# First block's shift and scale from VectorE's sums in place of TensorE's one-column matmuls, with a new order of all instructions

## The chip, the core and the metric

The kernel runs on one core of a Trainium2 chip. The core has five engines with a queue of instructions each: TensorE (PE in the profile, with PEld for its weight loads), VectorE (DVE), ScalarE (ACT), GpSimd (POOL) and SyncE (SP), which issues nearly all DMA transfers. An engine takes its instructions in the order in which they were issued and stops at one whose semaphores are not yet there; everything behind it on that engine waits too. The metric is the device time of one execution in microseconds (us); the time of the kernel before is the median of three runs.

## The reference: what is computed

One layer of a decoder, for a single sequence of 512 tokens with 1024 channels and one conditioning vector c, in float32:

```
mod = silu(c) @ ada_w + ada_b                 # 6 x 1024: shift, scale, gate, twice
sh1, sc1, g1, sh2, sc2, g2 = split(mod, 6)
h = rms_norm(x, g) * (1 + sc1) + sh1          # the modulated input of the mixer
y = hybrid_mixer(h)                           # RG-LRU branch and sparse attention
x = x + (1 + g1) * rms_norm(y)
h = rms_norm(x) * (1 + sc2) + sh2
y = square(relu(h @ w_ff1)) @ w_ff2           # 1024 -> 4096 -> 1024
x = x + (1 + g2) * rms_norm(y)
```

The change concerns the first two lines: how sh1 and sc1 are computed for the first 128 of the 1024 channels. Each is, per channel, a sum over 1024 products silu(c)[k] * ada_w[k, channel] and a bias.

## The kernel before

Every float32 weight is split into a high and a low part of the type fp32r (names hi_..., lo_...), the activations likewise (h, hl), and a float32 product is three fp32r matmuls into one PSUM bank: high by high, low by high, high by low. All matmuls are issued by one helper (L396), transposes by another (L400), ScalarE's operations at L407, those of VectorE and GpSimd at L441, loads on SyncE's queue at L483.

The order of the work is not that of the program text. The helpers only record each operation as a node, with the engines that could do it; `flush` then issues the nodes in the order that `PLAN` spells out, two characters a node. Where an operation can be done by more than one engine (a copy or an elementwise operation), `PLACE` says for each stage, letter by letter, which takes it: a for ScalarE, d for VectorE, p for GpSimd. Both strings are written out in the kernel. So each engine's queue, SyncE's with the loads too, has a fixed order across all stages. A load into a buffer that was used before waits until the last reader is through, and every load behind it on SyncE's queue waits with it.

The opening works in this order. `OPENING` loads the four tiles of x (128 tokens by 1024 channels each, 512 KB), six tiles of ada_w (512 KB, name p, from in_ada_a) and the first two weight blocks of the projection (384 KB, raw_a). The p tiles have six buffers, so the seventh load goes into the first one's buffer. TensorE runs 24 filler matmuls (stage WM) on x's first tile into a bank of the first wave, whose result nobody reads (name s). ScalarE squares and sums each x tile, GpSimd makes the reciprocal root, and x is scaled in column blocks of 128, 256 and 640 (stage XN; r<-r,stat in the profile). silu(c) lies as a column layout `sil` (128 x 8); eight float32 matmuls broadcast it over all 128 partitions into two PSUM banks (tp<-sil,ident), and two copies (the stage with the empty name in `PLACE`) make of them `silb`, 128 x 1024.

Then the eight blocks j of 128 channels follow in `first_wave`: `ada_sums(j)` gives the block's shift and scale as two columns `sa`; `ada_load(2)` loads two more ada_w tiles; four transposes turn the block of x; ScalarE makes h = scale * x + shift from the PSUM bank (for j = 0 in two halves of 256 tokens), once rounded to fp32r and once in float32 (pt), VectorE takes the difference hl; and 18 matmuls (stage MW: 3 terms by 6 column tiles of the projection) add it into six PSUM banks, f, f, s, s, pv, pv.

`ada_sums` has two forms. For j > 0 the two ada_w tiles lie transposed, channels on the partitions, and VectorE multiplies each with `silb` and sums along the row (tensor_tensor_reduce, shown as CUSTOM_DVE_ANT_0 p<-p,silb, with the read of its accumulator), followed by one small step for the scale. For j = 0 the two tiles lie the other way, and TensorE makes the sums: 16 float32 matmuls of one column for the shift and 16 for the scale, as the profile counts them (8 k-blocks, 2 records each), into the two banks pv that the wave uses later; a tensor_add and a scalar_tensor_tensor on VectorE (sa<-pv) finish them.

Behind the wave come the rest of the projections, the conditioning columns ar, the recurrent branch and the attention (to about 275 us), the output projection and residual, and the MLP in two passes over weights f and A, B (284 to 612 us).

Of the kernel before, what the change touches and what calls it, by code (L numbers as in the profile page):

```python
# [16 lines left out]
S = 512
D = 1024
NT = 4
KD = 8  # L20
# [75 lines left out]
    '2d372E2K2~2G3S2c2j2g2e2f382b2l2i333V3T2k39352r2h2n342/2m2q363W2*2p3X2%2o2-3*3!3U2,3x3#2<2]3c3Y2?2=3y3C3Z'
    '3I3$2:3a2{2@583d2^3O3F3D3z3b3%3e3h3&3J3n3+3P3(3L3i3o3,3R3)3t4#3k3/4H3?3u4%3:3q4F3{3@45463w3A473G3M484M2.'
    '3|3f4O494C3l3r4A3<4N4B3-4g3=4G4$4h4i4k4l4m4j4Q4^4&4n4P4+4o4,4-4]GY4(4.2+2>4~4S5L504)2;514*3]5K4/2[4_3~4{'
    '4d2_3^5Y3E413K3Q52425D3B5X5M4|4}59533H3j445E5h5A5B5C435F5H5G3N5g5J3p3v5O3g3m5I5N5S3;5$3[5P3s4b7%5T3.5R3>'
    '4a3_3}4J5Q5#5Z5U5V5a5b5i5j5k4I5-5W5l5m5d5n5o5p5q5,5r4X5s7&4V5t5u4K5e627)6;4c6-5v4L5w6<6.6/5x6=5y615z5f6d'  # L100
# [1709 lines left out]
```

## Time and profile before

| what | value |
|---|---|
| time, three runs | 627.72, 629.02, 629.98 us; median 629.02 |
| the profiled execution | 627.82 us, its span 626.0 us |
| mean granted TensorE clock in it | 0.991 |
| TensorE busy | 596.3 us (95%) |
| VectorE busy | 539.2 us (86%) |
| ScalarE busy | 346.1 us (55%) |
| GpSimd busy | 209.1 us (33%) |
| instructions in the profile | 9043 |

The span runs from the first to the last instruction; the time of the execution is a little longer. A row of a timeline gives the start and length of an operation in us, its engine and line, what it writes and reads, and in brackets the idle time of its engine just before it and what ended it. Operations of one engine overlap a little at their ends, so the distance from start to start is what one costs in a dense row of them, not the length.

### The profile page before, as it was taken

Reading aid. Unit: us, or ns where it says so; the run is one execution under the profiler, and the core shown is the slowest. Engines: PE = TensorE matmul, PEld = TensorE weight load, DVE = VectorE, ACT = ScalarE, POOL = GpSimd, SP = SyncE. Lnnn points to the kernel's source line nnn. Section 1 sums busy time; section 2 is a strip of 40 time slices with the busy share of each in tenths; the row PEclk is TensorE's granted clock in tenths of the full one; section 3 lists DMA queues with packets and bytes.
Section 4 is the critical chain, followed back from the end, with each engine's and each line's share of the span. In section 5 each row is a group of like instructions: output and inputs, shape, how many; then the busy total and the mean of one; then the engine's idle time right before and its main releaser. Section 6 shows DMA issues by size and latency. Waiting matters only on the chain.

```text
span 626.0 us, 9043 instructions
## 1 busy us (share of the span) xinstructions
PE 596.3 (95%) x3060; PEld 497.9 (80%) x3060; DVE 539.2 (86%) x1072; ACT 346.1 (55%) x696; POOL 209.1 (33%) x209
## 2 busy tenths in 40 slices
PE   7999999998999999989999999999999999999992
PEld 6888788966777898869887888888887888878881
DVE  5986988979999988988888968787688789999897
ACT  6654525698999999687251220322322247465563
POOL 5001301652663175453204547641351231000113
PEclk9999999999999999999999999999999999999997
DMA  8968895430503302015664334254544426756613
GB/s 351 416 250 318 320 299 191 131 136 1 202 2 129 141 2 102 1 35 176 229 222 168 115 133 137 101 169 157 180 135 147 155 69 204 238 179 202 198 56 134
DMA packets 29430, 102.15 MB, mean 163 GB/s; under 512 B 3268, under 2 KB 3524, under 8 KB 29384
## 3 DMA queue, kind: packets, MB, share of 16 engines
q1 hardware_dynamic: 29240, 101.50, 46.4%
q8 instruction: 24, 0.39, 0.3%
q14 instruction: 22, 0.18, 0.1%
q10 hardware_dynamic: 144, 0.07, 0.0%
HBM read 99.47 MB, written 2.10 MB: 162 GB/s over the span
## 4 chain that ended last, share of the span: by engine, by line
PE 73%; DVE 11%; DMA 6%; ACT 5%; issue 3%; DVEq 0%; SPq 0%; ACTq 0%
PE f L396 36%; PE s L396 14%; PE pv L396 13%; PE tp L396 7%; DMA ar<-in_ada_t 4%; PE tp L400 4%; DVE r L441 3%; ACT p L407 2%; DVE fT L441 2%; ACT r L407 2%; DVE ar L441 1%; DMA raw_A11l<-in_wd 1%; DMA raw_A10l<-in_wd 1%; DVE p L441 1%; DMA r<-in_x 1%
## 5 line engine op out<-in xcount | busy, mean ns | idle before, releaser
L396 PE MATMUL f<-h,hi_f 128*128 128x512 f32 x224 | 87.7, 392 | 0.0
L396 PE MATMUL f<-h,lo_f 128*128 128x512 f32 x224 | 87.2, 389 | 0.0
L396 PE MATMUL f<-h2l,hi_f 128*128 128x512 f32 x224 | 87.2, 389 | 0.0
L407 ACT ACTIVATE fT<-f 128x512 f32<-128x512 f32 x30 | 17.8, 594 | 71.2 <-PE f L396 71.2
L396 PEld LDWEIGHTS f<-h,hi_f 128*128 128x128 f32 x224 | 42.1, 188 | 8.8 <-issue 0.2
L396 PEld LDWEIGHTS f<-h2l,hi_f 128*128 128x128 f32 x224 | 42.0, 188 | 8.6
L396 PEld LDWEIGHTS f<-h,lo_f 128*128 128x128 f32 x224 | 42.0, 188 | 8.5
L396 PE MATMUL f<-hi_o,h 128*128 128x512 f32 x128 | 47.7, 414 | 0.0
L407 ACT ACTIVATE p<-p,mx 128x32 f32<-128x32 f32 (+4 forms) x96 | 45.1, 472 | 3.8 <-DVE mx L441 3.6
L441 DVE TENSOR_TENSOR lo_f<-raw_f,hi_f 128x1024 fp32r<-128x1024 f32 x29 | 40.1, 1383 | 6.9 <-ACT hi_f L407 6.6
L400 PE MATMUL tp<-ident,p 128*128 128x128 f32 x192 | 41.6, 273 | 1.9 <-DVE pt L441 0.9
L396 PE MATMUL pv<-pt,V 128*128 128x256 f32 x160 | 42.2, 316 | 1.1 <-ACT pt L407 0.7
L441 POOL TENSOR_SCALAR p<-p,den 128x32 f32<-128x32 f32 (+4 forms) x43 | 35.7, 863 | 18.5 <-DVE den L441 15.5
L396 PE MATMUL s<-K,Q 128*128 128x288 f32 (+4 forms) x128 | 38.4, 336 | 0.5 <-DVE Q L441 0.3
L441 DVE TENSOR_TENSOR pt<-tp,pt 128x512 fp32r<-128x512 f32 (+1 forms) x56 | 33.6, 609 | 3.3 <-ACT pt L407 1.9
L407 ACT ACTIVATE hi_f<-raw_f 128x1024 fp32r<-128x1024 f32 x24 | 24.9, 1056 | 18.7 <-PE f L396 13.0
L396 PEld LDWEIGHTS pv<-pt,V 128*128 128x128 f32 x160 | 27.8, 189 | 6.1 <-DVE pt L441 2.1
L396 PE MATMUL s<-r,fs 128*128 128x512 f32 x96 | 32.5, 389 | 0.0
L396 PE MATMUL pv<-r,fs 128*128 128x512 f32 x96 | 31.8, 391 | 0.4 <-DVE r L441 0.4
L400 PEld LDWEIGHTS tp<-ident,p 128*128 128x128 f32 x192 | 25.0, 140 | 7.8 <-issue 1.8
L396 PE MATMUL tp<-r,fs 128*128 128x512 f32 x96 | 30.6, 389 | 0.0
L441 DVE CUSTOM_DVE_ANT_0 ar<-ar,silb 128x1024 f32<-128x1024 f32 x16 | 21.6, 1352 | 6.4 <-DMA ar<-in_ada_t 6.4
(732 smaller groups left out, 1817.0 us busy)
## 6 DMA issues: line engine op xcount, KB each, us to landing
raw_f<-in_wf SPq DMA_DIRECT2D x32, 512.0 KB, 3.5
p<-in_ada_a SPq DMA_DIRECT2D x16, 512.0 KB, 8.0
ar<-in_ada_t SPq DMA_DIRECT2D x16, 512.0 KB, 4.4
ar<-in_ada_r SPq DMA_DIRECT2D x16, 512.0 KB, 4.0
r<-in_x SPq DMA_DIRECT2D x8, 512.0 KB, 4.6
raw_c<-in_wc SPq DMA_DIRECT2D x8, 512.0 KB, 5.2
raw_o<-in_wo SPq DMA_DIRECT2D x8, 512.0 KB, 6.4
raw_a<-in_wa SPq DMA_DIRECT2D x8, 384.0 KB, 7.5
```

The lines of the kernel that those rows point to most:

```text
L396: lambda: self.nc.tensor.matmul(out, lhs, rhs, start=start, stop=stop))
L400: self.issue("pe", 0.109, [out], [src], lambda: self.nc.tensor.transpose(out, src, ident))
L407: return "act", cost, lambda: self.nc.scalar.activation(out, src, func, scale=scale, bias=bias, **kw), func
L441: return eng, cost, lambda: fn(out, *args, **kw), None
```

## The change

`ada_sums` loses the branch for j = 0: the first block's shift and scale are two tensor_tensor_reduce and one small step on VectorE, like those of the other seven blocks. On the host the first two tiles of `ada_a` are laid out transposed like the others. The number of nodes goes from 4836 to 4821: sixteen matmul calls (32 records in the profile) and two VectorE operations fewer, three VectorE operations more.

`PLACE` and `PLAN` are made anew for the whole kernel. Counted over all free picks, ScalarE goes from 568 operations to 569, VectorE (with its fixed ones) from 938 to 961, GpSimd from 201 to 178. In the opening the two copies to `silb` go from VectorE to ScalarE, and of the twelve scalings of x six are ScalarE's, five VectorE's and one GpSimd's, where eleven were ScalarE's and one VectorE's. The new order puts on VectorE first the scale sum of block 0, then some scalings, the low part of the first weight block, the shift sum of block 0, and then the sums of blocks 1 and 2. The loads keep their order up to the fourth block of the next weights.

```
 PLACE = {
-    '': 'dd',
+    '': 'aa',
...
-    'XN': 'aaaaaadaaaaa',
+    'XN': 'paadaddddaaa',
...
 PLAN = (
-    '000O0P020Q0106400R0S0T0U0V0M074p4q084r0a0W0y040b4sGX4t090c030&0d0X0A554u0C4v054w0e4x0(0-4y0Y0H0N4z4!0D4:'
+    '000O0P020Q010M0R0S0T0N0U0V074a0B3:4b084c090a0y4d0W0A4e0C0b0&0c0X030d0e4f0z4g3}0-0H0Y4h044i0(0f054j0!0I4k'
...
         sa = const.tile([P, 2], F32, name=f"sa{j}")
         b, b1, pm = cols[:, V_AB + j:V_AB + j + 1], ab1[:, 8 + j:9 + j], cols[:, V_PM + j:V_PM + j + 1]
-        if j == 0:
-            w = [a.rearrange("p (k s q) -> p k s q", k=4, s=2) for a in ada[:2]]
-            to = [wave[4][:, 0:1], wave[5][:, 0:1]]
-            for k in range(KD):
-                for e in range(2):
-                    mm(to[e], w[k // 4][:, k % 4, e, :], sil[:, k:k + 1], k == 0, k == KD - 1)
-            dve("tensor_add", sa[:, 0:1], to[0], b)
-            dve("scalar_tensor_tensor", sa[:, 1:2], to[1], b1, pm, op0=ALU.add, op1=ALU.mult)
-        else:
-            for e, first in enumerate((b, 0.0)):
-                w = ada[2 * j + e]
-                dve("tensor_tensor_reduce", w, w, silb, 1.0, first, ALU.mult, ALU.add, sa[:, e:e + 1])
-            dve("scalar_tensor_tensor", sa[:, 1:2], sa[:, 1:2], b1, pm, op0=ALU.add, op1=ALU.mult)
+        for e, first in enumerate((b, 0.0)):
+            w = ada[2 * j + e]
+            dve("tensor_tensor_reduce", w, w, silb, 1.0, first, ALU.mult, ALU.add, sa[:, e:e + 1])
+        dve("scalar_tensor_tensor", sa[:, 1:2], sa[:, 1:2], b1, pm, op0=ALU.add, op1=ALU.mult)
         return sa[:, 0:1], sa[:, 1:2]
...
-    first = ada[:, :2 * D].reshape(KD, P, 2, KD, P)[:, :, :, 0, :]
-    ada_a = [first[k:k + 4].transpose(1, 0, 2, 3).reshape(P, 1024) for k in (0, 4)]
-    ada_a += [ada[:, e * D + j * P:e * D + j * P + P].T for j in range(1, KD) for e in range(2)]
+    ada_a = [ada[:, e * D + j * P:e * D + j * P + P].T for j in range(KD) for e in range(2)]
```

More of the change, by code (lines that the diff above doesn't have):

```diff
@@ L87 @@
-    'XN': 'aaaaaadaaaaa',
+    '': 'aa',
+    'AS': 'daapaaappdapaadapadpdppppapddapaapadpppadaddpdaadpdddaappadaapadppdadddpaappppppapppppppappdppap'
+        'appaaadpppapaaad',
+    'AV': 'aaaaadadddaddddaaddaaaaaaaaaaadaadadaaaaaaaaaaaadaaaaaad',
+    'AW': 'adaddaadpppddddd',
+    'DA': 'pdpddddadddpdddddddddppdddadddddpdadddddadppdappddddddpdddpappadpdpadpaddaddddddpadddpdpdddddpdd'
+        'ddddddpdppapdddapddddadddpapdddpaddppddddpdaddddaddaddddppddddapdddddddddaddaddd',
+    'DN': 'adadadadadadadadadddadadddadadadddadadadadadadadadadadadadadadadddppdddppddd',
@@ new lines @@
+    'FA': 'dddpddddpddd',
+    'RS': 'ppadddddadda',
+    'TH': 'daddaaddddddaaddddddaadpddddaadd',
+    'UP': 'ddppddpdddpddpddddpddpdddddddddd',
+    'VW': 'pdpddddddppdppppppp',
+    'WS': 'adadadadadadadadadadadapadadadapdpapadapddadddapadadadadaddaddadpadddddpaddaddadadaddadddddaddda'
+        'dddddaddapddaddadpaddadddaddadddddadddadpddpdddadaddddadpadddddpaddadpadddpddddddddaddddaddddadd'
+        'addadddaddddpdddddadaddaddaddddadadpaddaddadadaddaddadddddaddaddadddadadppadadddadadddadadddadad'
+        'ddadadddadadddddadddadadddadadddadadddadadddadadddadadddadadddadad',
@@ L96 @@
[L96 to L100, printed above, removed]
@@ new lines @@
+    '120q0%0^0r0s0t1U0u140|0v0}0+0w17131V0x181H1B0$1C1X1#151Y1E1Z1G1g1a1)1b1K1$1F1c1M1*1+1D1W1,161J1e1h1P1d1N'
+    '1Q1S1:1%0<1i1n1L1f1&1I1.1O1(2B271R1-1T1t1l2I1k1q061;2C1o2p1z2D1m261<2E1u1w1j1r1x1/291p1!2A1v2J1?1s1y281='
+    '2e2K2F1@1]1[2G2i1^2q1{1|1}242d2j1>22232N2k202f2H2g2l2:2;2m1~2h2-1_2L2r2n2O21252[2<2.2T2R2P2Q2X4@2=2o3G2M'
+    '2s2]2Z2S2u2W2/2U3D2^2>2Y2V3H2y2?3I2a3E2c3N2x2!2b2%3O2,302&2v3F3J2@3P3l2)3L2#3j2|363K2*3m2}3s3n3i343o3A33'
+    '393T3k3S4[3M3p2_313Y3t3q3Z3e3x3C3r3u3%3f4m3,403V3?374o3y3[3QGJ3&3b423-3@3h3_2t3W4]3]2w473{2$3!3c493^483|'
@@ new lines @@
+    '4R4S4T4n4V2z3v2(4W4A3#4*4X4)4U4p2+4Y4q4Z4r4C3*563)4E2{2~4B4t3/414u4N4v4w4/553<4s4:3;4x4+354,4D3B5J574;4-'
+    '4<4}4.4L3U5I4=4~4^4_4{50323=5S383R4|3>51523a543X3d5R593g3z3(535D7o583w5n7p3$5G5A3+3.5E5C5B5K4M5L5M7r5T44'
+    '5m5U5V4I5W5X5O5Y5H5v5Z5a5F5b4O5c5d5u435e5f6O5g5h465P6z5<5i5j5N456P6!6v5k4P5o5l6w6x6#4H5[5;5p7q6$4G6Q6+4F'
+    '5]5q685r676,6y6-6&5^4Q5_6G5{5|5Q4K6R5}6(4J5~5s606.616F5t62635w6S7$6b5x5y6a6)5z6*5!6/647%5+656j6T666%6<69'
+    '5,6A6B6C6D6U6E7-5#6V6W6i6X5$6H6I5%7;6;7L6Y5&5-6J7t6@6K6=7M5(5)6L6Z5*6:5.6c6[6d5/6N6e6|5:6>6M6f5=6g6{5>6h'
@@ new lines @@
+    '7C5?6?6]6k5@6^7D6l6_6m6n7N7&7k7Z7(787)777.6o7/6p7:7d6q7eGH7<7a6r7f7=7>7?6s7b7@7c7l7g7h7[7]7i7j6}7*867^6t'
+    '7u6~8G7m8O8P8H7v7_8I7+7{8M7w8K7|8Q708S8L7}718=8>728[7x8^738?748U8]9p857~758_80818~8N90768J7987GK91937A7z'
+    '8@7n897E7B8R7F8V8A6u9q7G8T8B7H9t8C7I7J928D7K7O958E7P968F7QGL8*949y7R7S9rG&7T8+9z7U8,8W978-9!8.8/9s8:G)8f'
+    '9u8;8g8h8i8X8j7V8k8l8<988b8{A99E8m8|8e8nG*8o8p8d8q8r7y8s999D8tG+8Y8u7s8}7!8ZAF7,9G8a7W9H8v8c8wG(9W9#AA7#'
+    '8x828y9X8z8!8#7X8$9c9I8%9Y9J9C9K9B9Z8&839LAG9d9M8(AH9N9e9O9PAD9a9g9h9f9i9Q9jAB9R9b9k9l9S9m9?AI9n9T9@Ag9A'
@@ new lines @@
+    '9o9F9~9v8)9[9UBwAh9w9V7Y9]9^9_AaAb9xAi9{A0BxA19$AcACAeA29%CMAE9}9&9(9)A39*AJ9+9,AKA5B^9-A4AwCNCO9|A$9.AN'
+    'CTAOBy9/HAALCUAdCV84AkAfAxB_9:A%Ca9;AlAmC8ARCbAnAQCcB{A!APCmASAyAT9<CnAoCoA&CtC9AjA6CuAUCvA7ApA}9=A;A(Cx'
+    'A~A8CyA#A?B4CzB2B6AVB0Aq88B3ArBeB5B1B7AzC!A<BfAsA)A=C#AMBAA>BCC+B8AtHBA@AWBgA*AuHMA/A.C$BhBuA:AXAvA-A^B;'
+    'BvAYA[HCA_CGB=A]A+B<A,AZA{BYHDCHA|BSBZBTBUBNB>BaBVC2BWCICBBbBXC4C3BcCFC6CCC5BOBmC7BiCDBdBnBjC,CKBkC&BoC('
+    'C-C/DGC:C;CEC<C=CPC>CSC)C@CJC[DHC]C^CLC_C{C|CfCQDIC}C~D0CWD1CZD2D3D4CXBlChD5BqCkBrBsD6D7CrC*9>ClD9CgDADB'
@@ new lines @@
+    'D8CeDnDCDoFSBtCsD&DDDEDtDFC%D(DJD)DKB9DLCiDfD*DMCYDNDOCpDgDSBDD+CdDTBBDUDjCqDuDrDVDhDWBEDpDPDXBpD,DlDYBF'
+    'DZCjBPD-DaDkCRDbDcC?DqDdDsD.D/DiBzB!DeC.B#EdD|DmEeEfBKD@DQBMEgBJD:D;FUB&D<DvBLB(B%D[D}BGEhDwCwEiEsEtBHB)'
+    'B*D#B-D=B+BILpD~EuFWE(D%D_B.E)E0E*D]GGB,ELEMCAD!E+B$E,ENLqEPE-E_G~ERFoEvESE{D$EQE|DxB/F3DzF4ETD{FYF5D>B:'
+    'FOEUBQFPBRFQD^D?H0E1FRB?EwE2EOB@B[FVE#EVDyE3H4EWE$EZEBDRE4E%EHH$HPECEcB]FCEzFDF-E5FZB|ExB}FEEIEaH%F6EJED'
+    'EbF7E6EXE7F.F/E8E9B~FAEAF8FpF=GuGvEKH8EEF:E>GwE?F!EFFTF#H5EjEGFXE@H&FuC0FvF>E.EkFyE/E:ElF;EYE;EmF$LrE[F@'
@@ new lines @@
+    'EnEoF+GFE<GiE]C1E=EpFaH6EyFwErFbGjE^FeFcFfFdFgFhEqGcGkGdFkFFFlGgFmG_G{E}FqF,FnFrGxFiFsF<GeF1G>GyFjGlF?F]'
+    'G?FtFzF^F_F{F|F}F9F2F~G]F[F&FBH(F(H)G|H*E&GzG0H1G@H9E!HaHbHmH+G^H,G8G1FGE~G9F)FHH-FJH2G}FKGAHeF*HnGBFLH.'
+    'GCG2HoHfH3GDG3G4FNHcG5IFFMHyG6HzHdH/H!G[G7I0IGGEHpGSGWI1GXGTGhGYGZHqGUHrGVGMGNGaHuGOGPH:HxGQGbH#G!FIHKGR'
+    'H;F0GfIJFxG,G#HNF%IKIHG$JDI2I4G-ILHOGmIrI5HwI%H7IlGnG%HLG.ImGsJEIIG:G;InJFIpGqG<IsG/I&GrG=ItI(I{HQHgI3HU'
+    'J6IuHVHhJGHRIqHiJHJIIoJ7HTHSJ8GtHWHEHFIvJ9H@HGHjJwJ2HkHXIwJAH[I$JBHYHlJxHJJyJCJzHZI|HtH<GoJ!HsJ%HHH^HIIB'
@@ new lines @@
+    'H_H=GpH{H]H>J#H?I6J$I7I}H|IAI8J&MgI9K9J0J(ICH}IMKAKBIDJ)H~MeIQKbJ*INJ+MWK2J3JeMYIEIRISIOJ4J1MZHvJkJfKcJg'
+    'IzIZIPJlITIUJ5K3JmIaIbIcIfMfK4IdJ|IgIhJiJ}IiIVIeKdIjKeI)JnKfMhJ]I-IWKgIkI*I~I.I+I,JhI/MXJ^JjI[I:KhJ~I;Ki'
+    'J_JoKjI!I=I>KkK1K5I?IYI]KTJ{I@JpIxKXI<JJI#KULDK0IXKYKVI^JKJSIyLEI_JvJsJTKxJUKZKyKWJYJLJVJMKzJtLFJWKaK(JZ'
+    'JNJOLSK#JPJaJuK)JXK|K!LTJbJRJ,LUJcK*J-J.LeK+J:JdK}L1LfK~L2K,J/J>JrKHJ?L3J;K-LaL5KIK<J<KJKKJ@L0LhJ=J[LiKL'
+    'KCL4LbLgK;LcKNKOKDKPK/LjLlKEKQJqLmLdJQK:LnKML:L;K6KRK7L>L?KpL<K8L@KSKlKmMNL=KqK=KnL[MOLoLGKGKoLHLIKrLkLJ'
@@ new lines @@
+    'KtKuKFKvMRKsK$LKMPK%K.KwL]MSK[K]LLLMK&K^LNLtL^LOMTLPL_LxMVLyL~LQLuMyK{LzK>L}LvLRM$L!M%MUK_LwL%L#M&L*MzM1'
+    'L+L,LVL&L-M!L(L)K?L$L.K@L6M0MBL/N2M|MCMDOaL7LYMFMGMELZL8MHL9MQM}MIN3M2N1OeM6MsM~MtM3ObMJMuMKM7MvMLMMM9LA'
+    'MwMnN4LBMAMoLWNdMxM4NhNiL|LCNeNlOfLXM<OiNjMjM@M[MkM=NfM>MpM)MaM(M*MlM+M,M8M?N*M]N.M-M^OjMbN0McN+M_M.L{M/'
+    'M:OcN/N,M;NEM#NPOdNQNLOgNFN-M{O7NRNMNNNSN:O&NTNGNOMrO(N5NVMqO)NUNWNZO*OkN6NHNXN7NYO+NANBNINJOlNaO8O,NbO-'
+    'O9NCN;OmO.NcNmOhNvOBO/OANwNKLsOCNnNgODNxMiN#NyOEN$NDNoMdN%O:NpNzN&PGNqPHN!N(PIPJO;NrPTM5N)N<N@N[N=N>N]N?'
@@ new lines @@
+    'OFN^O>O1N|N_PUO2N9O3N}NkN~O0N{O4N8PKNsO<PVOGPLO5O?OSOOOHPWNuOKOPO6OTOQPXOUORPYNtOLO=OWOVOsOXPZOIOYPaOMON'
+    'OtPbO@OZOuOvOnOyOwOzO!OoO#PMOxO$PcPNOpO{POO%P0O[P1O|O}OrP2P3PdPeP4PAPBO]PfPCPDO~O^PPPQP5P6PROJP7P8PSP9Mm'
+    'PuPEPqPrPvPsOqP<PgPwPtP=PFP$P%P>PxPyPhPzP!PkP#QAP&QBPjP?QCP@P(PiO_P)QEP*QDP+P[PlP]QFP^P,QGP_P{P|QIPmQOP-'
+    'QHP}P.QJP/P~QKPnP:PoQLP;Q(Q)Q*QMQ+Q0PpQiQjQ,QNQPQQQRQYQZQSQaQ-Q4QbQTQ]Q^Q3QVQ_Q{QcQ|Q1QUQ}Q2QdQ~QrQsQfQk'
+    'QtQuQ5QeQlQmQwQnQoQvQpQqQhQ6Q#QWQ$Q%QgQ.QXRAQ&Q7Q8QxR0RCQ/RBRDQ:Q;Q=Q<R4RERFRgQ>RhQzRiQ?R1RjQ@RGRkRlQ[Rm'
@@ new lines @@
+    'QyR2RnQ9RoRpQ!RqRrR3RsSHRtRuRHRvRwRxR+R,RJRLR-R.R/R5R:RIR;R<R=R~S0S1S2S3S4RKS5R6S6S7S8S9SASBSCSDT}SERVSF'
+    'SGSKSLSMR7SNT~SOSPR8RWSQSRSSSTSUU1SVSWR9SXSYSZSaSISbScSdSeU2SfSgShRMRNU0RORXRYRQRZSiSjU4SkRPSlSmSnSoRbSp'
+    'RRSqSrSsRaStRSSuSvRcSwSxRTSyRyRdRzR!ReR#SzS!RUR%S#R>S$U3R?R$S%S&R@R[RfS(U8R&S)R]S*S+S,SJR(S-R^S.S/S:R)S;'
+    'R_S<S=R*S>R{S?S@R|S[S]S^S_R}S{S|S}T>S~T0T1T2T/U9T3T?T4T5T6T7U5T8UAT9UBTATBUCTCTDTET@TFUETGUDTHT;TIU~URTJ'
+    'TKTLUST<UTTMTNUUV0T=UVU6TOUWT:UXUFTPU7TQUYT[V1TRTSTTUZTUTVUGUbTWUcTXUdTYUfT]VAUgULTZTaUhUjUkUMTbUlUnV5Tc'
@@ new lines @@
+    'UNTdUoVGTeUHTfUpUOTgThUqTiTjTkTlV2V6VBTmUPUyVaUzTnU!UIUQU#U$U%U(U)ToUaU*U+U,V7TpU-UeTqU.U/VbVCU:TrTsU;U<'
+    'TtUiU=VfU>U?UmU@U^TuVDV3UxTvVVTwVEUuTxTyV4TzU_UrT!T#UsVFUtUvT$VJU{VKWrUwU|VLT%T&T^VcWsT(VdUJVeVMVHVjUKVN'
+    'WwT)VkT*T_T+T,VOT-VlVgVmVnU&T.VoVqT{VrVhVsVPVvVwVxVIVzV!VQU[VZV#V(ViV)U}V*U]VRWGV+V,V-V;XOV.V<V=V>WHV?Xt'
+    'V@V[VpVSV]V^T|V_V{V|V~W0WxVTVtW1W3W4VWWIW5VuVUWJW8WXW9WAWBVyWCWDWRWyWEWSWTWUWtWuVXWvW!W#V:W$VYW%W&WKW(V}'
+    'W)W*W+WFW,W-W.W2W/W:W;V/WVWWW?W6W@W7W[W]W^XPW_WLW}W{V$W~X0X1XuX2X3X4X5X6XQX7X#X8WYX9WzWMXAXBXUXCWZXDXEXF'
@@ new lines @@
+    'XVXGW|XHXIXJWNXKWOXLX(WmXMX)X*YWX+X,YXX-X.WaX$X/X:X;WbX<V%X%X=X>X?X@X[X]Y#X&X^X}WcY$WdX~Y0Y1Y2XWY,Y3V&Y6'
+    'WqY7Y8Y9YAYBYCYDY-YEYFYGYHY4YIY.YJYKYLYMYNYZYOY/YPYYYQXRWeWfYRWnYSYTY:WoY;Y<WgZeY=Y>Z,ZfY?Y@XSXXY[Z?Y]Ya'
+    'Y^Z-Y_WhWiYUY{WjXNZ>Y|Y}WpY~XTWkYcWlZ0Z@XZZ1Z2Z6Z7YbZ[Z8XfZ9ZAZBZhZEZCZFXaY5YdXbZGZHXcZIXdW<ZJZKXeWPZLXg'
+    'YVXiXjXkXoZMZNZOYeXlamZPZQZiXmZgZRZSZTapZUZVZWWQZXXnZYXYZZZaZbZ]a}ZcXvZ^W=a>XwZ_anZ{ZjZ|a~Z}Z~a0Xxa1Zna2'
+    'b0a3ZDXya4a5Xha6a7Zka8Xsa9W>aAaEZlXza?aFaGaHaIaJawaMa|aKX!ZmaNXpasaOaPYhaQbuaRaSaTXqaUaVaWaXaYYiYnaZXrYj'
@@ new lines @@
+    'aaabacYkb|adaeafZdagahaiajYlb1Yfb2b3b4X_b5Ymb6b}X{b7b8YqYob9YrakYsYtc6bAYubBbCX|atbDbEaqYvV8Y%YpbFY&bGau'
+    'Y(Y)aobHYwbIY*bMc7Y!Y+Zpc5bNbOZqalZrc8ZsZtbxbPZubQarbRbyZybvbUbzYxZzbVbwbWbSZvbXbYbZb!baaLbbZ!bcYybdbebf'
+    'c$Yzbgd5bhbiZ#c+bjbkd6blbmZ$bnboc(dDbpZ%bqbrZ.bsc9cAcBbtcCcDcEZ3cFcGZ/V9Z4Z:dEcHcIb#cJbTcKZ;cLc%ZwcMZ<Z5'
+    'cNZ=cOdFcPcQaxcUcVc&dGcWZ&cXcYcZZxeDccaycdd:Z+ceb$cfZ(azeEcgcachcicjckZ)eLclcmcnd-Z*a!b%cocpc.a#b&cqa$cb'
+    'crcsctcua)cva%a*a+cwa,cxcyczdHaBa-dIdJdKdLdMYgdNdOdPa/dQdRdSa&dTeMdUdVdWa(a.dXa:dYeNa=dcddc!dea@c)a[avdf'
@@ new lines @@
+    'dgdhfLdkdidla]a;dmdndod.dpaCdqdraDdsdtc#dua<a^a_eOdjdvdwa{b.b(dxdydzd!d#c/d$d%d&Zob)d(d)bJd*b*ePc*eQb[eR'
+    'fUeSeTd/eUb+c,eVc-b,eWeXfVeYb-eZb/b;b<eabKb:ebecd+b=fMedeeb>efb?bLb@fTb~c0b{e?egekd;fWd=c1ele@c2b]emd,c3'
+    'enc4eoc:epb^c;esetgTd@eub_c<d>e~evewd?c=f}c>exe[eyg1eze!d<c?c^c_e]e#c{e$c@e%e&e(c|c}e)f0c~e*cRd7e+e,d0cS'
+    'e-d8e{eqe.d9dAc[e/cTdBe:e^e;ere<fXe=fYg8fZc]e|dCfagcd]d1fbd4d^d2d_d{fcd|fdfee_ffd3fgd}fhg4fie>fje2e3g2fk'
+    'gUfle4fme5fng3fogbe6d~e7fsdZfte0fueFe8f~fveGfwe1fxeHfyf!e9eCf#daf$f%gdf&eIf(eJf)dbgef*f+eAf,f-f.hCeKeBf/'
```

124 lines of the change are left out of this document (22 added, 102 removed).

## The prediction, made before the changed kernel ran

> **What bounds the kernel now.** I read the times of the engines first, then the table by stages, then the chain of waits, and last the rows of each engine around the change. The page of the profile:
>
> ```profile
> span 626.0 us, 9043 instructions
> PE 596.3 (95%) x3060; PEld 497.9 (80%) x3060; DVE 539.2 (86%) x1072; ACT 346.1 (55%) x696; POOL 209.1 (33%) x209
> ...
> PE 73%; DVE 11%; DMA 6%; ACT 5%; issue 3%; DVEq 0%; SPq 0%; ACTq 0%
> ...
> L407 ACT ACTIVATE fT<-f 128x512 f32<-128x512 f32 x30 | 17.8, 594 | 71.2 <-PE f L396 71.2
> ```
>
> TensorE is busy for 596.3 of 626.0 us and holds 73% of the chain that ended last. The profiled execution took 627.82 us, so 1.8 us lie around its span. The median of the three runs is 629.02; I work out a difference on the profiled execution and add it to the median. The three runs differ by 2.3 us among themselves, so 0.3% (1.9 us) is about what a measurement of this kernel tells from no change.
>
> The busy time by stages (columns: stretch, its length, then busy time and count of PE, PEld, DVE, ACT, POOL, the granted clock, the DMA share, GB/s):
>
> ```profile
> 10.36:18.61 8.25, 8.25 (x78) 8.25 (x76) 6.97 (x19) 6.99 (x14) 1.75 (x4) 1.00 1.04 421
> 18.61:46.15 27.54, 27.54 (x137) 22.25 (x136) 25.08 (x47) 16.75 (x24) 0.00 (x0) 1.00 0.83 323
> 46.15:100.00 53.85, 50.74 (x291) 43.00 (x291) 45.10 (x73) 22.60 (x37) 6.91 (x7) 1.00 0.85 303
> 100.00:275.00 175.00, 168.72 (x980) 139.75 (x980) 160.16 (x468) 154.32 (x390) 85.46 (x97) 1.00 0.24 85
> 275.00:284.00 9.00, 6.25 (x35) 5.81 (x36) 8.23 (x14) 7.85 (x12) 3.51 (x4) 0.81 0.21 65
> 284.00:612.00 328.00, 327.07 (x1516) 271.93 (x1516) 278.09 (x404) 127.69 (x200) 100.84 (x78) 1.00 0.48 161
> ```
>
> From 18.61 us, where the first projection matmul starts, to 46.15 TensorE has no gap at all, and VectorE is busy for 25.08 of 27.54 us. From 284 to 612 TensorE waits 0.9 us in all. It waits 3.1 us in 46 to 100, 6.3 us in 100 to 275, and 2.8 us in the hand-over to the MLP. The stretch of 8.25 us ahead of 18.61 looks full as well; the chain of waits shows with what (first its shares in 10.36 to 18.6, then two of its pieces with their start and length):
>
> ```profile
> by line: PE s L396 51.2%; PE pv L396 35.6%; PE tp L396 9.3%; PE tp L400 6.7%
> ...
> 12.03 0.22 PE tp L396 x2
> ...
> 45.91 0.24 PE s L396
> ```
>
> The pieces named pv are the 32 one-column matmuls that the change deletes, 0.356 x 8.24 = 2.9 us; the pieces named s are filler matmuls that nobody reads, and tp at L396 is the broadcast of silu, whose last piece ends at 12.25.
>
> **What is removed.** Those 2.9 us do not shorten the path by themselves. What the first projection waits for is the scaled and shifted block of x, made by ScalarE from the two sums:
>
> ```profile
> 15.98 0.49 ACT L407 ACTIVATE r<-r,stat 128x256 f32<-128x256 f32 x1
> 17.38 1.02 ACT L407 ACTIVATE h<-tp,sa 128x256 fp32r<-128x256 f32 x2 [0.91 <-DVE sa L441]
> ```
>
> ```profile
> 12.09 0.29 DVE L441 TENSOR_SCALAR r<-r,stat 128x128 f32<-128x128 f32 x1
> ...
> 12.57 0.68 DVE L441 COPY silb<-tp 128x512 f32<-128x512 f32 x1
> ...
> 13.24 0.95 DVE L441 TENSOR_TENSOR lo_a<-raw_a,hi_a 128x768 fp32r<-128x768 f32 x1
> 14.11 1.28 DVE L441 CUSTOM_DVE_ANT_0 p<-p,silb,vecs 128x1024 f32<-128x1024 f32 x1
> ...
> 15.31 1.22 DVE L441 CUSTOM_DVE_ANT_0 p<-p,silb 128x1024 f32<-128x1024 f32 x1
> 16.46 0.08 DVE L441 DVE_READ_ACCUMULATOR2_ANT sa<- 128x1 f32 x1
> 16.93 0.16 DVE L441 TENSOR_TENSOR sa<-pv,vecs 128x1 f32<-128x1 f32 x1 [0.39 <-PE pv L396]
> ...
> 17.08 0.21 DVE L441 SCALAR_TENSOR_TENSOR sa<-pv,ab,vecs 128x1 f32<-128x1 f32 x1
> ```
>
> Before, VectorE makes the second block's two sums while TensorE makes the first block's; VectorE then waits 0.39 us for TensorE, and both sums are there at 17.08+0.21 = 17.29.
>
> **What is added in the opening.** The two copies of the broadcast silu go to ScalarE. A 128x512 copy takes 0.59 us there (the fT row), the broadcast matmuls end at 12.25 (I take the same for the new order), so silb is whole at about 12.25+0.1+0.6 = 13.0 instead of 12.57+0.68 = 13.25. From there the new order puts on VectorE, ahead of the first block's scale and shift: the scale sum (15.31 to 16.46: 1.15), two column blocks of 128 (12.09 to the next start about 0.2 each), one of 256, some small operations, the scale's last step: about 1.1 together; then lo_a (13.24 to 14.11: 0.87), then the shift sum (14.11 to 15.31: 1.20) and the read of its accumulator, 0.08. That is 13.0+1.15+1.1+0.87+1.20+0.1 = 17.4, 0.1 later than before. The order of ScalarE then has one half of h, a 256-column block of x (0.49), and the other half of h, where before both halves follow each other: 0.5 more. So the first projection starts at about 18.61+0.1+0.5 = 19.2: **+0.6 us**, and TensorE stands idle for about 2.9+0.6 = 3.5 us that the deleted matmuls and the delay leave. Column blocks of 256 and 640 on VectorE are not in the trace; they lie between the 0.2 net of 128 columns and the 0.87 net of 768, and I take 0.3 and 0.5, since 256 is nearest to the first and 640 nearer to the second but without its second operand. With the block of 256 and the small operations at their least the start moves by +0.3, with the block at 0.87 by +1.2.
>
> **What is added in the first wave.** VectorE gets all sums of the first block. From the start of lo_a at 13.24 to the end of the last difference of h:
>
> ```profile
> L441 DVE CUSTOM_DVE_ANT_0 p<-p,silb 128x1024 f32<-128x1024 f32 x7 | 8.5, 1220 | 0.3 <-DMA p<-in_ada_a 0.3
> L441 DVE TENSOR_TENSOR h<-pt,h 128x512 fp32r<-128x512 f32 x8 | 5.4, 686 | 0.8 <-ACT pt L407 0.4 <-ACT h L407 0.4
> ```
>
> ```profile
> 44.11 0.69 DVE L441 TENSOR_TENSOR h<-pt,h 128x512 fp32r<-128x512 f32 x1 [0.42 <-ACT pt L407]
> ```
>
> it took 44.80-13.24 = 31.56 us, of which 0.39+0.3+0.8 = 1.5 were waits and 0.3 the two operations on pv: 29.8 of work. The change adds 1.15+1.20+0.13 for sums and last step and 1.2 for four column blocks that lay ahead or on ScalarE: 33.4, though about 0.2 of small operations move out; I take 33.2. From 13.0 it ends at 46.2 if it never waits, 1.4 later. The bank that the next stage reads first is done at 45.91+0.24 = 46.15; moved by 0.6 its last matmuls start near 46.5, after 46.2. So it just fits, with 0.3 us to spare, and the wave ends 0.6 later. The bounds: +0.3, if the start is at its least, and +1.8, if VectorE waits 1.5 us again (46.2+1.5+0.3-46.15).
>
> **What is moved behind.** 22 more of the free operations go to VectorE and 23 fewer to GpSimd (201 to 178), ScalarE gets one more. An operation of 128x512 costs 0.69 on VectorE (the h row) and twice that on GpSimd:
>
> ```profile
> L441 POOL TENSOR_TENSOR r<-r,r 128x512 f32<-128x512 f32 x9 | 12.2, 1360 | 17.2 <-DVE r L441 9.4 <-ACT r L407 7.8
> ```
>
> That is at most 22 x 0.69 = 15 us more of VectorE over the whole span. Most lie in the MLP passes, where VectorE has 328.00-278.09 = 50 us free and TensorE waits for 0.9 in all: nothing there. In attention the new picks take VectorE's work away rather than add some (scores 29 to 25, values 20 to 15), and ScalarE has 20 us free. If that cover were gone, the same 15 us over stages in which TensorE is busy for 547 of 557 us would show by the share of its waits, 10/557, so as 0.3 us, and all of them only if each fell into a wait. The order of TensorE is displaced by some 46 places at most, the marks of the stages (last matmul of the scores, first of the MLP) by under 20; the gain or loss is bounded by the 3.1+6.3+2.8+0.9 = 13 us of idle time in the rows above. I take 0, with a ninth of them, 1.5 us, either way, since the marks hardly move.
>
> **Sum.** Profiled: 627.82+0.6 = 628.4. At the median: 629.02+0.6 = **629.6**.
>
> **Rivals.** (1) Slower: VectorE becomes the bound of the wave. The load of the seventh column tile goes into the buffer of the first, and its release moves:
>
> ```profile
> 14.64 0.33 SPq L483 DMA_DIRECT2D p<-in_ada_a  x1
> ```
>
> ```profile
> p<-in_ada_a SPq DMA_DIRECT2D x16, 512.0 KB, 8.0
> ```
>
> ```profile
> 39.00:42.00 3.00, 3.00 (x17) 2.40 (x16) 3.00 (x6) 1.84 (x3) 0.00 (x0) 1.00 0.05 15
> ```
>
> Before, TensorE's reads free it for an issue at 14.64; after, the shift sum does at 17.4, and all loads behind it on the queue of SyncE (the eighth tile, three blocks of weights) start 2.8 us later. With 8.0 us from issue to landing the eighth tile is there at 17.6+8.0 = 25.6. The new order wants it on VectorE after four sums, two last steps, two differences of h, one lo_a and the block of 640: 17.4+4.7+0.3+1.2+0.9+0.5 = 25.0. Before, it was already waited for by 0.3. So 0.6 to 0.7 late, and the same again for the tiles whose buffers these free, 1.4; with the other waits of before after 17.4 (0.3+0.8) VectorE ends at 46.2+2.5 = 48.7 and the bank with it: +2.6, **631.6**. It decides as soon as these waits pass the spare 0.3 us. Against it: transfers had a pause of their own in 39 to 42 (share 0.05), so late tiles can catch up, and the queues are empty when they start again, so a landing takes less than 8.0.
>
> (2) Slower: TensorE's idle time in the opening lowers its clock. The trace shows that case at the hand-over to the MLP:
>
> ```profile
> 276.05 0.39 PE L396 MATMUL pv<-h,hi_f 128*128 128x256 f32 x1 [1.08 <-ACT hi_f L407]
> ...
> 278.08 0.39 PE L396 MATMUL pv<-h,lo_f 128*128 128x256 f32 x1 [1.41 <-DVE lo_f L441]
> 278.30 0.28 PE L396 MATMUL pv<-h,hi_f 128*128 128x256 f32 x1
> 278.42 0.29 PE L396 MATMUL pv<-h2l,hi_f 128*128 128x256 f32 x1
> ...
> 279.95 0.45 PE L396 MATMUL pv<-h2l,hi_f 128*128 128x256 f32 x1 [0.30 <-DVE h2l L441]
> 280.20 0.42 PE L396 MATMUL pv<-h,lo_f 128*128 128x256 f32 x1
> 280.42 0.42 PE L396 MATMUL pv<-h,hi_f 128*128 128x256 f32 x1
> ```
>
> After 2.5 us of waits the spacing is 0.22 instead of 0.12, and the stretch's granted clock 0.81 of 9 us, so 0.19 x 9 x 2 = 3.4 us at half speed, 1.7 us lost. The same after the opening's 3.5 us of idle time gives 0.6+1.7 = +2.3, **631.3**; it decides if the slow stretch falls on projection matmuls rather than on fillers. Against it: the idle time is in two parts with 2 us of fillers between, and a slow stretch that begins early costs only fillers. [...]
>
> (3) Faster: the new order closes a gap elsewhere, above all the hand-over, where 1.08+1.41 of waiting and the 1.7 of slow clock go together: -4.2+0.6, **625.4**. For it: the order is new everywhere, and fewer results come from GpSimd, which takes twice as long. Against it: the operations ahead of hi_f and lo_f are the same ones in the new order.
>
> (4) The deleted matmuls were on the path after all, since the chain runs through them: -2.9+0.6, **626.7**. Against it: the rows above have the shift sum at 17.4 whatever TensorE does.
>
> **Chances.** Forecast 0.48, (1) 0.18, (2) 0.10, (3) 0.16, (4) 0.08. The forecast's own range is 627.8 (+0.3-1.5) to 631.1 (+0.6+1.5). With (1), (2) and (4) inside, and (3) and the far side of (1) left out, the range is 626.0 to 632.2. Faster by over 0.3% (under 627.1): (3), (4) and a tenth of the forecast, 0.28; slower (over 630.9): (1), most of (2) and a few in a hundred of the forecast, 0.28; the rest, 0.44, within.
>
> **What would show it.** Right: no pv matmul ahead of the first projection, that one at about 19.2, TensorE idle for 3 to 4 us ahead of it, VectorE without waits until 46, the bank's end near 46.8, TensorE's idle time behind within 1.5 us of before. Wrong: VectorE waits for in_ada_a of over 1 us (1), a matmul spacing of 0.4 in the wave (2), no waits for hi_f and lo_f (3), a start ahead of 18 us (4).

## The result and the profile after

The changed kernel takes 633.56 us (median of 19 runs, 627.87 to 638.76) against 629.53 us for the kernel before (19 runs, 626.86 to 632.18). The ratio is 1.0061, with a 95% interval of 1.0044 to 1.0079 (it leaves out the run of 638.76 us, which counts as a slow one): slower by some 4 us, where no measurable change was forecast (629.6, range 626.0 to 632.2).

The execution that was profiled took 629.67 us, less than most. Its page and its table by stages (the columns are those of the prediction):

```profile
span 627.9 us, 8977 instructions
PE 592.5 (94%) x3028; PEld 494.1 (79%) x3028; DVE 552.3 (88%) x1097; ACT 343.4 (55%) x697; POOL 170.8 (27%) x186
```

```profile
10.36:18.61 8.25, 6.05 (x51) 5.68 (x49) 5.60 (x15) 5.04 (x11) 2.39 (x7) 1.00 1.00 406
18.61:46.15 27.54, 25.93 (x127) 20.54 (x126) 27.54 (x53) 16.88 (x26) 0.00 (x0) 1.00 0.84 315
46.15:100.00 53.85, 51.68 (x297) 44.16 (x296) 45.39 (x70) 23.24 (x38) 5.29 (x6) 1.00 0.88 311
100.00:275.00 175.00, 166.71 (x965) 138.93 (x964) 162.21 (x466) 152.75 (x391) 76.28 (x89) 1.00 0.24 84
284.00:612.00 328.00, 327.37 (x1525) 272.96 (x1526) 284.32 (x428) 125.30 (x193) 73.77 (x63) 1.00 0.49 161
```

The 32 one-column matmuls are gone, TensorE is idle in the opening instead (6.05 of 8.25 us busy ahead of 18.61), and VectorE has no gap in the wave (27.54 of 27.54). From 100 to 275 TensorE waits 8.3 us, 2.0 more than before. The opening is late as forecast, and by more (timeline rows of TensorE, then of VectorE, then of ScalarE behind the wave):

```profile
15.89 0.44 PE L400 MATMUL tp<-ident,r 128*128 128x128 f32 x2 [2.20 <-DVE r L441]
...
19.59 0.50 PE L396 MATMUL pv<-h,hi_a 128*128 128x512 f32 x1 [0.93 <-ACT h L407]
```

```profile
13.79 1.23 DVE L441 CUSTOM_DVE_ANT_0 p<-p,silb 128x1024 f32<-128x1024 f32 x1 [2.62 <-ACT silb L407]
...
46.45 0.69 DVE L441 TENSOR_TENSOR h<-pt,h 128x512 fp32r<-128x512 f32 x1
```

```profile
47.95 1.20 ACT L407 ACTIVATE r<-s 64x512 f32<-64x512 f32 x2 [1.52 <-PE s L396]
```

The first projection starts at 19.59 (before 18.61), VectorE's last difference of h ends at 47.14 (before 44.80), and the first bank is ready at 47.9 (before 46.15). This execution took 1.85 us more than the one profiled before, so the opening can explain it. It does not explain the median. The mean granted clock of the 19 runs goes from 0.975 to 0.994, and the longest have the low clocks: 629.37 us at 0.992, 637.24 at 0.975. In between the two go together less closely: one run took 632.32 us at 0.994.

### The profile page after: what moved, and what is told of

It reads as the page before. It is cut to its first block, busy times and chain, and to the rows that moved or that the text cites. A ratio compares the mean times of both kernels' runs of the same rounds, so it can differ in the third digit from the quotient of the medians.

```text
span 627.9 us, 8977 instructions
## 1 busy us (share of the span) xinstructions
PE 592.5 (94%) x3028; PEld 494.1 (79%) x3028; DVE 552.3 (88%) x1097; ACT 343.4 (55%) x697; POOL 170.8 (27%) x186
## 4 chain that ended last, share of the span: by engine, by line
PE 51%; DVE 3%; DVEq 0%; issue 0%
PE f L396 28%; PE s L396 8%; PE pv L396 8%; PE tp L396 7%; DVE fT L441 2%; DVE ar L441 0%; DVE fs L441 0%; PE tp L400 0%; DVE lo_f L441 0%; DVE stat L441 0%; DVEq L1795 0%; DVEq L441 0%
## 5 line engine op out<-in xcount | busy, mean ns | idle before, releaser
L441 POOL TENSOR_SCALAR p<-p,den 128x32 f32<-128x32 f32 (+4 forms) x40 | 34.3, 868 | 16.7 <-DVE den L441 16.5
L407 ACT ACTIVATE hi_f<-raw_f 128x1024 fp32r<-128x1024 f32 x20 | 21.0, 1055 | 27.6 <-DMA raw_f<-in_wf 19.7
L396 PEld LDWEIGHTS s<-K,Q 128*128 128x128 f32 x128 | 23.1, 189 | 7.7 <-issue 2.5
```

What stands on the lines that cost most here:

```text
L396: lambda: self.nc.tensor.matmul(out, lhs, rhs, start=start, stop=stop))
L407: return "act", cost, lambda: self.nc.scalar.activation(out, src, func, scale=scale, bias=bias, **kw), func
L441: return eng, cost, lambda: fn(out, *args, **kw), None
```

## The experiments

Every kernel was timed beside the kernel before on the same chip; ratios are to that.

**The changed kernel again.** No edit.

> The changed kernel once more, unaltered. Its 19 runs go from 627.87 to 638.76 us with mean granted clocks from 0.994 to 0.975, its profiled one was one of the fast ones (629.67, 0.992). Clock theory (TensorE is idle in the opening in 2 to 3 us pieces and the granted clock falls in some executions): median near 633.5, the slower the run the lower its clock, and if this profile is of such a run, matmuls at half pace somewhere in the first 30 us, about 3 us lost by each 0.005 of mean clock. Order theory (the new order behind the first wave loses the time): median near 633.5 too, with the half pace or the idle time somewhere behind 46 us.

Measured: 637.85 us (633.5 expected), ratio 1.0119 (1.0085 to 1.0154), clocks of 0.975 to 0.987. This time the profiled execution is one of the long ones, 639.15 us at 0.977. Its table in short stretches, against the same of the quicker execution (last fence):

```profile
72.00:76.00 4.00, 2.23 (x14) 1.58 (x12) 3.92 (x5) 1.69 (x4) 1.33 (x1) 1.00 0.78 269
76.00:80.00 4.00, 4.00 (x15) 3.61 (x16) 3.82 (x7) 0.87 (x2) 0.00 (x0) 0.50 0.89 313
80.00:84.00 4.00, 4.00 (x15) 3.52 (x15) 3.08 (x6) 0.00 (x0) 0.00 (x0) 0.50 0.91 306
84.00:88.00 4.00, 4.00 (x17) 3.31 (x16) 3.25 (x5) 1.06 (x1) 0.00 (x0) 0.72 0.91 277
```

```profile
75.00:77.50 2.50, 1.50 (x6) 1.44 (x7) 2.46 (x4) 1.85 (x4) 0.00 (x0) 0.70 0.82 279
...
137.50:140.00 2.50, 2.50 (x9) 1.89 (x8) 0.63 (x8) 2.23 (x11) 0.40 (x2) 0.50 0.01 3
140.00:142.50 2.50, 2.50 (x13) 1.76 (x13) 0.92 (x7) 1.51 (x2) 0.14 (x1) 0.83 0.00 0
160.00:162.50 2.50, 2.12 (x8) 1.67 (x9) 2.44 (x6) 2.47 (x4) 0.00 (x0) 0.76 0.00 0
290.00:292.50 2.50, 1.93 (x11) 1.70 (x10) 2.35 (x5) 2.50 (x7) 1.91 (x2) 0.71 0.21 51
```

```profile
76.00:80.00 4.00, 4.00 (x25) 3.54 (x24) 2.96 (x5) 0.00 (x0) 0.00 (x0) 1.00 0.84 261
```

The third number from the end is the granted clock. It is 0.50 from 76 to 86.2, and again for about 3.4 us at 137.4, 161.3 and 291.0; the quicker execution runs the same work at 1.00 (25 matmul records in 4 us instead of 15). So most of the time is lost to TensorE's clock, and none of that in the first 46 us here. Ahead of the long stretch and of the second one TensorE waits, and VectorE and GpSimd show why (TensorE, VectorE, GpSimd):

```profile
67.71 0.50 PE L396 MATMUL f<-h,lo_x 128*128 128x512 f32 x1 [1.49 <-DVE lo_x L441]
...
76.00 0.77 PE L396 MATMUL f<-h,hi_x 128*128 128x512 f32 x1 [1.77 <-DVE Q L441]
...
136.06 0.37 PE L396 MATMUL s<-K,Q 128*128 128x288 f32 x1 [1.54 <-DVE mx L441]
```

```profile
65.28 1.23 DVE L441 CUSTOM_DVE_ANT_0 ar<-ar,silb 128x1024 f32<-128x1024 f32 x1 [1.98 <-DMA ar<-in_ada_t]
...
71.19 3.23 DVE L441 CUSTOM_DVE_ANT_0 ar<-ar,silb 128x1024 f32<-128x1024 f32 x1
...
74.46 1.39 DVE L441 SCALAR_TENSOR_TENSOR Q<-f,Q 64x512 fp32r<-64x512 f32 x2
...
132.98 2.48 DVE L441 TENSOR_SCALAR p<-p,den 128x256 f32<-128x256 f32 x1
...
135.38 0.41 DVE L441 CUSTOM_DVE_ANT_1 p<-s,tab 128x256 f32<-128x256 f32 x1
```

```profile
70.67 2.66 POOL L441 TENSOR_TENSOR lo_x<-raw_x,hi_x 128x1024 fp32r<-128x1024 f32 x1 [18.14 <-ACT hi_x L407]
...
132.94 2.37 POOL L441 TENSOR_TENSOR lo_g<-raw_g,hi_g 128x1024 fp32r<-128x1024 f32 x1 [1.82 <-ACT hi_g L407]
```

A sum that takes 1.2 us takes 3.23 while GpSimd makes a low part, and a scaling of 128x256 takes 2.48. The first ends 1.1 us after GpSimd's operation (71.19+3.23 against 70.67+2.66), the second 0.15 us after it, as if their work began when GpSimd's was done. Why it begins only then these rows do not show; the runs below with a low part moved test whether the GpSimd operation is what it waits for. What stands behind these two on VectorE (Q, and the maxima mx, the row p<-s,tab) frees the PSUM banks that TensorE waits for.

Of the 9.5 us between the long and the quick execution 1.9 are there ahead of the half pace: Q starts on VectorE at 74.46, against 72.52 in the quick one. A load for ar came late here (1.98 us of waiting against 0.52), lo_x behind it too, and TensorE waited 1.49 us for that at 67.71.

The kernel before has the first of the two blocked operations as well, but not the second (VectorE and GpSimd, then TensorE):

```profile
68.27 2.37 POOL L441 TENSOR_TENSOR lo_x<-raw_x,hi_x 128x1024 fp32r<-128x1024 f32 x1 [17.91 <-ACT hi_x L407]
...
68.41 3.32 DVE L441 CUSTOM_DVE_ANT_0 ar<-ar,silb 128x1024 f32<-128x1024 f32 x1 [0.60 <-DMA ar<-in_ada_t]
...
124.74 2.42 POOL L441 TENSOR_TENSOR lo_g<-raw_g,hi_g 128x1024 fp32r<-128x1024 f32 x1
...
124.89 0.41 DVE L441 CUSTOM_DVE_ANT_1 p<-s,tab 128x256 f32<-128x256 f32 x1
```

```profile
73.30 0.47 PE L396 MATMUL f<-h,hi_x 128*128 128x512 f32 x1 [0.76 <-DVE Q L441]
```

The sum takes 3.32 us beside lo_x0 there too, yet TensorE waits only 0.76 us for Q. Beside lo_g1 stand maxima, which read a PSUM bank and keep their 0.41 us.

**The changed opening with the old rest, and the old opening with the new rest.** `PLAN` is cut behind the wave's last matmul (after 458 nodes of the new order, after 471 of the old); the nodes left over follow in the other order, and `PLACE` goes with each node. In outline:

```
-PLAN = new[:458] + new[458:]
+PLAN = new[:458] + [n for n in old if n not in new[:458]]

-PLAN = old[:471] + old[471:]
+PLAN = old[:471] + [n for n in new if n not in old[:471]]
```

> The changed opening (all that is issued up to the last matmul of the first wave, with its engine picks) followed by all remaining instructions in the order and with the picks of before. If the opening alone costs the time (late start, or its idle time and the clock): 632.5 to 634, ratio 1.005 to 1.007. If the order behind the wave costs it: 629.5 to 631, ratio 1.000 to 1.002, the 1 us of the later start only.

> The opening of before with the 32 one-column matmuls, followed by all remaining instructions in the new order and with the new picks. If the opening alone costs the time: 629 to 630.5, ratio 0.998 to 1.001. If the order behind the wave costs it: 632 to 633.5, ratio 1.004 to 1.006.

Measured: 629.89 us, ratio 1.0017 (0.9999 to 1.0034), for the new opening with the old rest; 635.12 us, ratio 1.0079 (1.0050 to 1.0108), for the old opening with the new rest. The new order behind the wave costs the time, and more than the 1.004 to 1.006 expected. The opening costs about 1 us, though the interval reaches no change. With the old rest the only half pace among matmuls in the trace lies at the hand-over at 281, as before; with the new rest and the old opening it lies at 73 to 83, 134 to 138, 158 and 288.

**Fillers in the opening.**

```
-WARM = 24
+WARM = 40
```

`PLAN` gets the 16 new nodes as well.

> The changed kernel with 16 more filler matmuls in the three idle stretches of TensorE ahead of the first projection (2 at 5.5 us, 10 at 13.5, 4 at 18.5), nothing else changed. Clock theory with the opening as the place: clocks back to 0.990 or more in most runs, median 629.5 to 631. If the opening's idle time has nothing to do with it: 633 to 634 as before the fillers, with clocks down to 0.98.

Measured: 633.71 us, ratio 1.0077 (1.0049 to 1.0104), clocks from 0.977 to 0.993. The fillers do not bring the time back, and half pace comes at 75 to 82 and 157 to 160 all the same. Ahead of the first of these TensorE waits 1.69 us for a load of raw_c in this trace and 0.38 for Q, so not every such gap comes from the blocked sum. Whether they gained anything against the changed kernel beside them (1.0119) is open, as the intervals meet.

**Two low parts on VectorE.** In `PLACE`, two letters p of the changed kernel become d, those of lo_x0 and lo_g1 in the first row of the stage WS; for lo_x0 alone, only the first of them:

```
-    'WS': 'adadadadadadadadadadadapadadadapdpapadapddadddapadadadadaddaddadpadddddpaddaddadadaddadddddaddda'
+    'WS': 'adadadadadadadadadadadadadadadapdpapadadddadddapadadadadaddaddadpadddddpaddaddadadaddadddddaddda'
```

> The changed kernel with two picks altered and the order kept: the low parts lo_x0 and lo_g1 of two weight blocks (128x1024 each) on VectorE instead of GpSimd. In the slow trace of the changed kernel both run on GpSimd for 2.4 to 2.7 us while a VectorE operation beside them takes 3.23 instead of 1.2 and 2.48 instead of 0.4, TensorE then waits 1.77 (for Q, at 74) and 1.54 (for mx, at 134.5), and half pace follows for 10.2 and 3.4 us. Theory (GpSimd blocks VectorE, TensorE's gap lowers the clock): both gaps under 0.9, no half pace at 76 to 86 and 138 to 141, clocks of 0.985 and more, median 629.5 to 631. If the gaps come from the order by itself: gaps as before, 633 to 636. If the clock falls by another cause than these gaps: gaps shorter, half pace there all the same, 632 to 635.

> As the run with two picks altered, but only lo_x0 (the gap at 74). By the same theory the 10 us of half pace at 76 to 86 go, which cost 5 us where they come, and the 3.4 us after the wait for mx stay: 630 to 632. If only the second place matters: 633 to 635.

Measured: both moved 629.39 us, ratio 1.0032 (1.0014 to 1.0050), all clocks 0.988 to 0.993; lo_x0 alone 631.02 us, ratio 1.0063 (1.0036 to 1.0090). With both moved the same operations have their plain lengths, and the gaps are short (VectorE, then TensorE):

```profile
70.83 1.23 DVE L441 CUSTOM_DVE_ANT_0 ar<-ar,silb 128x1024 f32<-128x1024 f32 x1 [0.32 <-DMA ar<-in_ada_t]
...
126.75 0.34 DVE L441 TENSOR_SCALAR p<-p,den 128x256 f32<-128x256 f32 x1
```

```profile
74.54 0.50 PE L396 MATMUL f<-h,hi_x 128*128 128x512 f32 x1 [0.69 <-ACT r L407]
...
130.10 0.30 PE L400 MATMUL tp<-ident,p 128*128 128x128 f32 x1 [0.89 <-DVE pt L441]
```

The sum takes 1.23 instead of 3.23, the scaling 0.34 instead of 2.48, TensorE waits 0.69 and 0.89 instead of 1.77 and 1.54, and the only half pace left among matmuls in this trace is at 152, behind a wait for ScalarE of 1.7 us that the kernel before has too (1.9).

**The four side by side on one chip.** The changed kernel, lo_g1 alone, both low parts, and both low parts with the opening of before.

> The changed kernel again, on the chip and beside the runs of the variants of this call, so that they can be compared with it directly: 633 to 638, ratio 1.006 to 1.012, clocks from 0.975 to 0.992.

> Only lo_g1 on VectorE: the wait of 1.54 for mx at 129 to 136 shrinks to under 0.9, the 1.0 to 1.8 us wait for Q at 74 stays and with it, in part of the executions, the 10 us of half pace. If the two places add up as the theory has it, the time lies between the changed kernel and the one with both picks moved, 631 to 635, and the gain by the first place (5 us where it comes) is the larger.

> Both low parts on VectorE, beside the changed kernel: 629.5 to 631, ratio 1.002 to 1.004, clocks 0.987 and more; 3 to 6 us under the changed kernel in the same call. If the difference between the calls so far was one of chips, it is under 2 us.

> The opening of before with its one-column matmuls, the rest in the new order, both low parts on VectorE. If the two costs add up (opening 0.17%, gaps behind it the rest): ratio 1.000 to 1.002, 628 to 629.5. If the new order costs something beside the two gaps: as with both moved, 1.003 or more.

| kernel | median us | ratio to before (95%) | mean clock |
|---|---|---|---|
| changed | 637.58 | 1.0147 (1.0126 to 1.0167) | 0.977 |
| lo_g1 on VectorE | 632.41 | 1.0061 (1.0040 to 1.0083) | 0.987 |
| lo_g1 and lo_x0 on VectorE | 629.84 | 1.0028 (1.0005 to 1.0052) | 0.990 |
| the same with the old opening | 628.49 | 1.0000 (0.9983 to 1.0018) | 0.989 |

Two letters take 7.7 us off the changed kernel. The difference in mean clock, (0.990 - 0.977) x 634 = 8 us, is enough for all of it. lo_g1 alone takes off 5.2 of the 7.7, against the expectation that lo_x0 is worth more. In the trace of lo_g1 alone TensorE still waits 1.56 us for Q, but only 3.4 us at half pace follow (76.3 to 79.7), not 10.2. The old opening takes off another 1.3, and nothing is left.

The changed kernel's own loss differs between its three sets of runs (1.0061, 1.0119, 1.0147); why low clocks were rarer in the first is open. There the clock does not account for all of the 4 us either: its mean over the 19 runs is 0.986, that of the kernel before is 0.989 in each of the later sets, and (0.989 - 0.986) x 634 is 1.9 us. The late opening and the waits themselves are left for the rest; no run divides it between them.

**The edit alone in the old order.** The order and picks of before without the 32 matmuls, the two sums and the last step of block 0 put right behind the second copy of silb (in outline):

```
-PLAN = old, with nodes 84 to 101 where they stood
+PLAN = old without them; behind the second silb copy: scale sum, shift sum, last step
```

> The edit alone: the order and all picks of before, without the 32 one-column matmuls and their two VectorE operations, and the first block's scale sum, shift sum and last step put on VectorE right behind the second copy of silb, ahead of lo_a. Sums ready at 13.25+1.15+1.20+0.1+0.13 = 15.8 instead of 17.29, first projection near 17.1, VectorE's last difference of h at 45.5 to 47. If the loss lies in the new order behind the wave alone: 628 to 630, ratio 0.998 to 1.001. If the sums on VectorE cost what the wave cannot hide: 630.5 or more.

Measured: 628.88 us, ratio 1.0019 (0.9996 to 1.0042). The edit alone makes no difference that can be told. Its first projection starts at 18.25 and not near 17.1, behind fillers that run at half pace:

```profile
15.01 3.48 PE L396 MATMUL s<-r,ident 128*128 128x128 f32 x16
...
18.25 0.47 PE L396 MATMUL s<-h,hi_a 128*128 128x512 f32 x1
```

```profile
10.36:18.61 8.25, 5.79 (x37) 5.55 (x36) 7.83 (x20) 7.38 (x15) 1.72 (x4) 0.79 1.03 420
```

The granted clock of that stretch is 0.79, with TensorE busy for 5.79 of the 8.25 us; the quick execution of the changed kernel had 6.05 and kept 1.00. Yet ScalarE reads the wave's first bank at 46.19, as before (46.17), so the wave took this up.

This execution also has 10.2 us at half pace from 52.4 to 62.6, which was not expected. In the 3.4 us ahead TensorE waits at most 0.84 us, but from 50.27 on it runs 26 matmul records of 64 columns in a row. So half pace came here without a long wait. The mean clock of this execution is 0.976 and its time 630.59 us, so a low mean clock does not by itself make a long time.

**A third low part, with the old opening.** lo_g0 is moved too, on top of the last row of the table.

> As the run with the old opening and two low parts moved (1.0000 of before), and a third one, lo_g0, on VectorE too. There lo_g0 ran on GpSimd for 2.77 us, a VectorE operation of 128x32 beside it took 2.35 instead of about 0.3, the bank behind it (V, then eg) came late, and TensorE waited 1.21 us at 116. If the blocking is the cause of this wait too: it shrinks to under 0.5, about 0.8 us are gained directly and some in the clock, ratio 0.996 to 0.999, under both kernels. If the 1.2 us more of work on VectorE cost as much: 1.000 to 1.002.

Without the third move (VectorE, GpSimd, TensorE), and with it (VectorE, TensorE):

```profile
114.13 2.35 DVE L441 TENSOR_SCALAR p<-p,den 128x32 f32<-128x32 f32 x1
...
113.68 2.77 POOL L441 TENSOR_TENSOR lo_g<-raw_g,hi_g 128x1024 fp32r<-128x1024 f32 x1 [1.82 <-issue]
...
117.08 0.39 PE L396 MATMUL f<-hi_v,h 128*128 128x280 f32 x1 [1.21 <-ACT eg L407]
```

```profile
112.77 0.22 DVE L441 TENSOR_SCALAR p<-p,den 128x32 f32<-128x32 f32 x1
...
116.71 0.39 PE L396 MATMUL pv<-pt,V 128*128 128x256 f32 x1 [0.78 <-DVE pt L441]
```

Measured: 627.36 us, ratio 0.9986 (0.9970 to 1.0002). The blocked scaling takes 0.22 instead of 2.35, and the wait for eg is gone; 0.78 of another wait comes in its place, so less than the forecast 0.8 us is gained directly. The median is the lowest of all, 1.1 us under before, but the interval reaches 1: this version equals or slightly beats the kernel before, and clearly beats the changed one.

## Why the prediction was wrong

**The step that failed** is "what is moved behind": "I take 0, with a ninth of them, 1.5 us, either way, since the marks hardly move". In its place the runs show some 5 us: 635.12 us (1.0079) for the old opening with the new rest. The prediction looked at places in TensorE's order, counted the picks that change hands, and priced them by their own length. It did not look at what each operation meets beside it. Neither low part changed hands: both are GpSimd's before and after. Beside lo_g1 the new order put a scaling, held up to 2.48 us, with maxima behind it that TensorE needed at once. Beside lo_x0 the same sum is held up before and after, but the new order left TensorE less to do meanwhile. From the start of the sum it had matmuls for 3.0 to 3.4 us in five traces of that order and then waited 1.02 to 1.90 us for Q; before it had them for 4.1 us and waited 0.76. Moving the two low parts took 637.58 us to 629.84.

Idle time of 13 us was taken as the bound of gain and loss. It is no bound: in the long execution the clock added a loss that is longer than the gap (1.77 us of waiting, then 10.2 us at half pace, so 5.1 us by their length; from Q to lo_g0 the long execution falls back by 4.6 us against the quick one).

**What is removed:** right. The matmuls covered a wait, and taking them out gained nothing.

**What is added in the opening:** right in kind, +0.98 at the first projection instead of +0.6. The term that was too small is the end of the broadcast of silu, "I take the same for the new order": the broadcast starts at 6.62 (before 6.58), but 22 filler records stand between its first and last piece, where before 8 fillers and 8 of the deleted records did, so silb was whole at 13.76 instead of 13.0. From there the working held: 13.79 to the last sum's end at 18.0 is 4.2 us, as summed (4.4).

**The first wave:** VectorE's load was right (13.79 to 47.14 is 33.4 us, forecast 33.2), without a wait, and the bank came 1.8 late instead of 0.6. End to end the opening costs 0.17% or 1.1 us (new opening, old rest; the interval is 0 to 0.34%), within the bounds given for it, +0.3 to +1.8.

**Rival 1**, VectorE waiting for late tiles: no. Its wave has no such wait, late loads or not.

**Rival 2**, the clock: right in kind, in the wrong place. It was looked for where TensorE lost matmuls. There it comes in some executions and costs little: lo_x0 alone had it at 17.0 to 20.4 and took 628.37 us. The loss lies at 76 to 86 and at 137, behind waits that the new order made or stretched.

**Rival 3** did not come: the hand-over still has waits of 1.06 us for hi_f, 0.56 for lo_f and 0.91 for h2l (0.30 before), though the quick execution runs it without half pace. **Rival 4** is refuted by the start at 19.59.

Not tried: fillers in the two gaps themselves, since no PSUM bank is plainly free there. That the gap, and nothing that comes with it, lowers the clock rests on the runs in which it was shortened (waits of 0.69 and 0.89 us with both low parts moved, and no half pace behind them); the edit alone had one fall with no wait over 0.84 us ahead of it.
